# Loading the first six modulation pieces of each mixer into idle activation slots

## The chip, the core and the metric

The kernel runs on one core of one Trainium2 chip. A core has TensorE (PE in the profile; PEld is its weight load), VectorE (DVE), ScalarE (ACT), GpSimd (POOL) and SyncE (SP), each working through its own instructions in order; SP issues nearly nothing but DMAs. The metric is the device time of one execution in microseconds. Three runs of the kernel before gave 1124.48, 1122.46 and 1122.72 us: a median of 1122.72.

## The reference, cut to what matters

Two layers over 256 tokens of width 1024. Each has a mixer of three branches and an MLP, and each of these is modulated by six vectors (shift, scale and gate, for mixer and MLP) that come from one conditioning vector `c`:

```python
mod = jax.nn.silu(c) @ ada_w + ada_b
sh_m, sc_m, gt_m, sh_f, sc_f, gt_f = [t[:, None, :] for t in jnp.split(mod, 6, axis=-1)]

h = rms_norm(x, g_pre_mix) * (1.0 + sc_m) + sh_m
proj = h @ w_in
...
y_ret = jax.nn.silu(rg) * ret.reshape(B, S, RET_V)
y_lru = jax.nn.gelu(ly) * rg_lru(u, w_a, b_a, w_x, b_x, lam)
...
merged = g[:, :, 0] * (y_ret @ ret_w_o) + g[:, :, 1] * (y_lru @ lru_w_o) + g[:, :, 2] * (y_fox @ fox_w_o)
x = x + gt_m * rms_norm(merged @ w_out, g_post_mix)
h = rms_norm(x, g_pre_mlp) * (1.0 + sc_f) + sh_f
f = jnp.square(jax.nn.relu(h @ w1)) @ w2
return x + gt_f * rms_norm(f, g_post_mlp)
```

All is float32. A product with the 256 tokens is done on PE as three products of rounded parts (high x high, high x low, low x high). The product `silu(c) @ ada_w` has one row only and is not done on PE: DVE multiplies a tile of `ada_w` by `silu(c)` and sums it.

## The kernel before

**Pieces.** The weights come in pieces of 1 MiB (1024 x 256 numbers), each as two halves of 512 KiB, in the order of the list `ORDER`. A weight piece ("gemm") is loaded as two `wraw` tiles (`raw_half`, five slots in turn); ACT rounds each half to its high part (line 240) and DVE subtracts to get the low part (line 241), both into a `wpair` tile, of which there are four, that is two pieces. PE then runs 48 matmuls on it (lines 369 to 371). A modulation piece ("ada") is loaded through the same five `wraw` slots, and DVE sums each half in one instruction (line 301, `ada_sum`); a small add of the bias follows (line 297).

**Order in the mixer.** `mix_order` gives the weight pieces of a mixer; its end is rg x4, g1, w_r x4, g1, ly x4, then the last 28: fq, w_l x4, fv x4, fq x3, fk x4, g2 x4, w_f x4, w_o x4. In this document they are counted from 0 at the first of these `fq`, and from 0 within a name (`w_l0` to `w_l3`; `fq1` to `fq3` are pieces 9 to 11 of the 28). `weight_order` and its `spread` put the modulation pieces between them, evenly from the piece that stands `MIXR[l][0]` before the end to the one `MIXR[l][1]` before it. Layer 0 has 12 of them in its mixer (gt_m, sc_f, sh_f, four each), layer 1 has 8 (sc_f, sh_f). Before, layer 0 puts 12 pieces after pieces 6 to 18 of the last 28, and layer 1 puts 8 after pieces 8 to 18.

**What sets the time of a load.** `prefetch` keeps two weight pieces ahead of PE and runs the modulation steps that stand between them. All loads leave through SP's one queue, in order; a load waits on SP until the reader of its slot is done, and holds what is behind it. The framework's scheduler may move instructions of an engine against each other where data allows it, unless they are pinned with `keep_in_program_order`.

**Activation slots.** T1 to T10 are big activation tiles with changing tenants (`U(tag, ...)`). In the mixer T5 holds the retention output `ro_o` (read last in `ret_gate`), T6 `lru_u` (read last in `gelu_gate`), T7 `lru_t` and T8 `lru_a` (read last in `recurrence`). From `fk` on, T5 and T6 hold the keys `fkh` and `fkl`, T7 and T8 the output of that attention, `yfh` and `yfl`. Between the two tenants they are idle. In the opening, T slots already serve as homes for raw pieces (tile `wfirst`).

**PSUM.** The result of a piece lands in one of two banks of the pool `pg`; it is emptied by ACT and DVE (for `fv`, `fq` and `fk`: a rounding on ACT, then a subtraction on DVE into `fvl`, `fql` or `fkl`) before the piece after the next can start. The modulation columns that a norm needs are collected in `rcols` shortly before `w_f` ends.

Of the kernel before, what the change touches and what calls it, by code (L numbers as in the profile page):

```python
# [10 lines left out]
F32 = mybir.dt.float32  # L11
# [3 lines left out]
ALU = mybir.AluOpType  # L15
PSUM = bass.MemoryType.PSUM
KH = 4
# [16 lines left out]
P = 128  # L34
# [7 lines left out]
C = 256  # L42
# [5 lines left out]
PARTS = {'sh_m': 0, 'sc_m': 1, 'gt_m': 2, 'sh_f': 3, 'sc_f': 4, 'gt_f': 5}  # L48
# [21 lines left out]
def mix_order(l):  # L70
    first = 'g0 g0 g0 g0 lx lx g1 lx g1 lx lru' if l == 0 else \
            'rv rv rv rv rq rk g0 rq rk g0 lx g0 lx g0 lx g1 lx lru g1'
    rest = 'rg rg rg rg g1 w_r w_r w_r w_r g1 ly ly ly ly fq w_l w_l w_l w_l fv fv fv fv fq fq fq fk fk fk fk ' \
           'g2 g2 g2 g2 w_f w_f w_f w_f w_o w_o w_o w_o'
    order = first.split() + rest.split()
    return [(n, order[:i].count(n)) for i, n in enumerate(order)]


def mlp_order():
    w1 = lambda g: [('w1', 4 * g + c) for c in range(4)]  # L80
    w2 = lambda g: [('w2', 4 * g + c) for c in range(4)]
    return w1(0) + w1(1) + w2(0) + w1(2) + w2(1) + w1(3) + w2(2) + w2(3)
# [4 lines left out]
    return name in ('rv', 'w_o', 'w2') or (name == 'w1' and cix < 4)  # L87


MIXR = ((22, 8), (20, 8))  # L90
MLPR = ((5, 28), (5, 15))


def weight_order():
    order = [(n, 0, k) for k in range(KD) for n in ('ada_row', 'row')]

    def spread(l, gem, ada, lo, hi):
        at = [lo + (hi - lo) * i // max(len(ada), 1) for i in range(len(ada))]
        for i, (n, c) in enumerate(gem):
            order.append(('gemm', l, n, c))  # L100
            while at and at[0] <= i:
                at.pop(0)
                order.append(ada.pop(0))
        assert not ada

    for l in range(L):
        n = len(mix_order(l))
        parts = [(l, p) for p in ('gt_m', 'sc_f', 'sh_f')][l:]
        spread(l, mix_order(l), [('ada',) + p + (c,) for p in parts for c in range(4)], *(n - i for i in MIXR[l]))
        parts = [(l, 'gt_f')] + [(i, p) for i in range(l + 1, L) for p in ('sc_m', 'sh_m', 'gt_m')]  # L110
        spread(l, mlp_order(), [('ada',) + p + (c,) for p in parts for c in range(4)], *MLPR[l])
    return order


ORDER = weight_order()


@with_exitstack
def trunk_kernel(ctx, tc, x, c, vec, con, ffw, wts, out):
    nc = tc.nc  # L120
# [5 lines left out]
    sp = ctx.enter_context(tc.tile_pool(name="sp", bufs=2))  # L126
# [5 lines left out]
    V, A, T = nc.vector, nc.scalar, nc.tensor  # L132
# [4 lines left out]
    sir = cpool.tile([P, D], F32, name="sir")  # L137
# [11 lines left out]
    def vc(l, name):  # L149
        o, w = VEC[name]  # L150
        return vsb[:, l, o:o + w]
# [57 lines left out]
    pos = [0]  # L209

    def raw_half(i, extra=None):
        n = C if extra is None else C + NH_F
        t = wp.tile([P, KH, n], F32, name="wraw", tag="wraw", bufs=NRAW)
        src = wts[pos[0], i]
        if extra is None:
            nc.sync.dma_start(t.rearrange("p k c -> p (k c)"), src)
        else:
            nc.sync.dma_start(t[:, :, :C], src.rearrange("p (k c) -> p k c", k=KH))
            nc.sync.dma_start(t[:, :, C:], extra[:, i * KH:(i + 1) * KH, :])
        return t  # L220
# [25 lines left out]
    def load_split(l, name, cix):  # L246
        with ExitStack() as stack:
            if (name, cix) in LATE:
                for i in behind.pop(l, ()):
                    stack.enter_context(tc.issue_after(i))  # L250
            return split_of(l, name, cix)

    def split_of(l, name, cix):
        parts = []
        for i in range(2):
            t = early.pop(0) if early else raw_half(i, ffw[l] if (name, cix) == ('fv', 0) else None)
            n = t.shape[-1]
            if (name, cix) in SLOTS:
                own = SLOTS[name, cix][i]
            elif name in ('w1', 'w2') and (name, cix) < ('w2', 12):  # L260
                own = SPARE_SLOTS[spare[0] % len(SPARE_SLOTS)]
                spare[0] += 1
            else:
                own = PL
            broad = wide(name, cix)
            if own:
                hi, lo = halves_of(up.tile([P, 2 * D + SLOT_PAD], F32R, name="wown", tag=own), broad, 0 if broad else PHASE)
            else:
                hi, lo = split_tiles(broad, n)
            split(t, hi, lo)  # L270
            parts.append((hi, lo))
        pos[0] += 1
        if wide(name, cix):
            return [(parts[k // 2][0][:, k % 2, :], parts[k // 2][1][:, k % 2, :]) for k in range(KH)]
        return [(parts[k // KH][0][:, k % KH, :], parts[k // KH][1][:, k % KH, :]) for k in range(KD)]
# [20 lines left out]
    def mod_bias(l, o, n, src):  # L296
        V.tensor_tensor(mods[l][:, o:o + n], src, vc(l, 'ada_b')[:, o:o + n], ALU.add)

    def ada_sum(t, m):
        t = t.rearrange("p k c -> p (k c)")  # L300
        V.scalar_tensor_tensor(t, t, 0.5, sir, ALU.mult, ALU.mult, accum_out=m)  # L301

    def ada_step(l, part, cix):
        m = sp.tile([P, 2], F32, name="mcol")
        for j in range(2):
            ada_sum(raw_half(j), m[:, j:j + 1])
        pos[0] += 1
        mod_bias(l, PARTS[part] * 8 + 2 * cix, 2, m)

    ahead = []  # L310

    def prefetch(n=2):
        while len(ahead) < n and pos[0] < len(ORDER):
            o = ORDER[pos[0]]
            if o[0] == 'gemm':
                ahead.append((o[1:], load_split(*o[1:])))
            else:
                ada_step(*o[1:])

    def weight(l, name, cix):  # L320
        prefetch(3 if name in DEEP else 2)
        key, w = ahead.pop(0)
        assert key == (l, name, cix), (key, l, name, cix)
        return w
# [104 lines left out]
    def U(tag, shape, dt, name, other=False):  # L429

        o, n = PHASE * other, math.prod(shape[1:])
        t = up.tile([P, 2 * D + SLOT_PAD], dt, name=name, tag=tag)[:, o:o + n]
        dims = {c: k for c, k in zip("abc", shape[1:])}
        return t.rearrange(f"p ({' '.join(dims)}) -> p {' '.join(dims)}", **dims)
# [25 lines left out]
    def first_rows():  # L460
# [38 lines left out]
        def row_sums(k):  # L499
            m = sp.tile([P, 2], F32, name="mrow")  # L500
            for j in range(2):
                ada_sum(raws[2 * k][j], m[:, j:j + 1])
            return m
# [181 lines left out]
              'w_l': 1.7, 'fq': 2.4, 'fv': 2.4, 'fk': 2.4, 'g2': 3.0, 'w_f': 1.2, 'w_o': 1.0}  # L685

    def mixer(l, nm, h=None, rvp=None, qkp=None):
        hh, hl = h or nm.h

        def G(name, i, x=None, natural=False):  # L690
            prefetch(3 if name in DEEP else 2)
            side(BUDGET[name])
            w = weight(l, name, i)
            ps = pa.tile([P, 2, S], F32, name="ps", tag="a") if name in LONG else None
            return (gemm_n if natural else gemm)(w, *(x or (hh, hl)), ps)
# [151 lines left out]
        if rvp:  # L847
            for j in range(2):
                for t in range(2):
                    rv_evac(rvp[t][j], (2 * j, 2 * j + 1), (t, t))  # L850
                if j == 0:
                    prefetch(1)
        else:
            def rv_quad(ps, t, j):
                rv_evac(ps.rearrange("p (h c) -> p h c", h=2), (2 * j, 2 * j + 1), (t, t))
                return lambda: None

            first_quad(l, 'rv', nm, rv_quad)
# [281 lines left out]
    for l in range(L):  # L1140
        nm = mlp(l, mixer(l, nm) if l else mixer(l, None, *first_rows()))
# [101 lines left out]
```

## Time and profile before

| what | us |
|---|---|
| median of three runs | 1122.72 |
| the profiled execution, its own time | 1122.77 |
| span of the profiled execution, first to last instruction | 1121.0 |
| loads of 512 KB into `wraw`, issue to landing, median | 4.3 |
| line 301 on `wraw` tiles, 82 instructions | 100.0 |
| line 241 on `wpair` tiles, 286 instructions | 347.4 |

The profile shows one execution. "Busy" is the time that an engine's instructions cover; matmuls are pipelined, so that their durations (278 ns) overlap and one starts every 113 ns or so. A row of the timeline gives start, duration, engine and line, operation, output<-inputs and shapes, and in brackets how long the engine had been idle and what ended that. In the table of waits a row gives who waited for whom, the total in us, how many times, and the longest.

### The profile page before, as it was taken

The page shows a single profiled execution, that of the slowest core. Times are in us where ns is not written, and L with a number is a line of the kernel's source. Part 1 is how long each engine was busy: PE and PEld are TensorE (multiplying, and loading weights), DVE is VectorE, ACT ScalarE, POOL GpSimd, SP SyncE. Part 2 cuts the span into 40 slices and gives each one's busy share as a digit, 9 for nine tenths or more (in the row PEclk, how much of TensorE's full clock was granted, in tenths as well). Part 3 has the DMA queues.
Part 4 walks back from the last instruction along what each step waited for, and adds up shares of the span by engine and source line. Part 5 has one row for each costly group of instructions (what it writes and reads, how often), then busy time and mean ns, then how long its engine had stood idle before and what let it go on. Part 6 is the DMA issues. An engine that isn't in the chain of part 4 may idle for free.

```text
span 1121.0 us, 20568 instructions
## 1 busy us (share of the span) xinstructions
PE 1099.2 (98%) x8208; PEld 1037.1 (93%) x8208; DVE 870.5 (78%) x1324; ACT 617.4 (55%) x924; POOL 47.0 (4%) x62
## 2 busy tenths in 40 slices
PE   8999999999999999999999999999999999999997
PEld 7999999998899889989879999999999997989986
DVE  5998788878797789888487768887878778866543
ACT  5686595644355546445455657755445655544441
POOL 1001000000000110000030010000000003000000
PEclk9999999999999999999999999999999999999999
DMA  9954646678886569998735455566678584886541
GB/s 364 407 181 158 195 137 214 194 248 294 286 266 222 188 213 335 338 333 306 278 136 188 139 185 186 164 213 198 235 267 284 184 283 134 281 276 195 197 156 59
DMA packets 74284, 255.43 MB, mean 228 GB/s; under 512 B 10108, under 2 KB 12492, under 8 KB 74188
## 3 DMA queue, kind: packets, MB, share of 16 engines
q1 hardware_dynamic: 74188, 254.12, 66.5%
q8 instruction: 64, 1.05, 0.4%
q14 instruction: 32, 0.26, 0.1%
HBM read 253.00 MB, written 1.09 MB: 227 GB/s over the span
## 4 chain that ended last, share of the span: by engine, by line
PE 73%; DVE 9%; DMA 8%; issue 4%; ACT 3%; POOL 1%; SPq 0%; DVEq 0%; POOLq 0%; ACTq 0%
PE ps L371 22%; PE ps L369 21%; PE ps L370 21%; DMA wraw<-in_wts_dram 8%; DVE wpair L241 3%; DVE wraw L301 2%; ACT wpair L240 1%; POOL rs_v L198 1%; ACT junk L450 1%; POOL rs_r L199 1%; PE rvp L369 1%; PE rvp L370 0%; PE qkp L370 0%; PE qkp L371 0%; PE qkp L369 0%
## 5 line engine op out<-in xcount | busy, mean ns | idle before, releaser
L241 DVE TENSOR_TENSOR wpair<-wraw,wpair 128x1024 fp32r<-128x1024 f32 (+1 forms) x286 | 347.4, 1220 | 76.6 <-ACT wpair L240 74.7
L240 ACT CAST wpair<-wraw 128x1024 fp32r<-128x1024 f32 (+1 forms) x286 | 298.5, 1049 | 192.6 <-PE ps L371 128.7
L369 PE MATMUL ps<-hh,wpair 128*128 128x256 f32 x1312 | 364.4, 278 | 3.6 <-DVE fvl L701 2.6
L371 PE MATMUL ps<-hh,wpair 128*128 128x256 f32 x1312 | 362.9, 277 | 0.1
L370 PE MATMUL ps<-hl,wpair 128*128 128x256 f32 x1312 | 362.7, 276 | 0.0
L369 PEld LDWEIGHTS ps<-hh,wpair 128*128 128x128 f32 x1312 | 246.4, 188 | 4.7 <-DVE fvl L701 3.0
L371 PEld LDWEIGHTS ps<-hh,wpair 128*128 128x128 f32 x1312 | 246.3, 188 | 0.3 <-DVE wpair L241 0.3
L370 PEld LDWEIGHTS ps<-hl,wpair 128*128 128x128 f32 x1312 | 246.3, 188 | 0.2
L301 DVE SCALAR_TENSOR_TENSOR wraw<-wraw,sir 128x1024 f32<-128x1024 f32 x82 | 100.0, 1221 | 40.2 <-DMA wraw<-in_wts_dram 40.0
L241 DVE TENSOR_TENSOR wown<-wraw,wown 128x1024 fp32r<-128x1024 f32 x72 | 87.5, 1221 | 26.7 <-ACT wown L240 26.3
L240 ACT CAST wown<-wraw 128x1024 fp32r<-128x1024 f32 x72 | 74.8, 1048 | 55.9 <-DMA wraw<-in_wts_dram 30.3
L369 PE MATMUL ps<-wpair,mih 128*128 128x512 f32 x144 | 56.3, 391 | 0.0
L370 PE MATMUL ps<-wpair,mih 128*128 128x512 f32 x144 | 56.1, 389 | 0.0
L371 PE MATMUL ps<-wpair,mil 128*128 128x512 f32 x144 | 56.0, 389 | 0.0
L369 PE MATMUL ps<-wpair,hh 128*128 128x256 f32 (+1 forms) x144 | 45.6, 317 | 0.0
L370 PE MATMUL ps<-wpair,hh 128*128 128x256 f32 (+1 forms) x144 | 45.4, 316 | 0.0
L371 PE MATMUL ps<-wpair,hl 128*128 128x256 f32 (+1 forms) x144 | 45.4, 315 | 0.0
L369 PE MATMUL ps<-hh,wown 128*128 128x256 f32 x160 | 44.2, 276 | 0.0
L371 PE MATMUL ps<-hh,wown 128*128 128x256 f32 x160 | 44.2, 276 | 0.0
L370 PE MATMUL ps<-hl,wown 128*128 128x256 f32 x160 | 44.2, 276 | 0.0
L369 PE MATMUL ps<-wown,mih 128*128 128x512 f32 x112 | 43.7, 390 | 0.0
L370 PE MATMUL ps<-wown,mih 128*128 128x512 f32 x112 | 43.6, 389 | 0.0
(348 smaller groups left out, 2303.3 us busy)
## 6 DMA issues: line engine op xcount, KB each, us to landing
wraw<-in_wts_dram SPq DMA_DIRECT2D x440, 512.0 KB, 4.3
wfirst<-in_wts_dram SPq DMA_DIRECT2D x28, 512.0 KB, 10.2
rows<-drow SPq DMA_DIRECT2D x10, 512.0 KB, 6.1
xs<-in_x_dram SPq DMA_DIRECT2D x2, 512.0 KB
out_dram<-xs SPq DMA_DIRECT2D x4, 256.0 KB, 2.0
csb<-in_con_dram SPq DMA_DIRECT2D x1, 768.0 KB
csb<-in_con_dram SPq DMA_DIRECT2D x1, 256.0 KB, 9.6
vsb<-in_vec_dram SPq DMA_DIRECT2D x1, 152.0 KB, 6.5
```

The lines of the kernel that those rows point to most:

```text
L198: pin(nc.gpsimd.tensor_scalar(v, part, rest, None, ALU.add))
L199: nc.gpsimd.tensor_tensor(r, v, mhalf[:, :1], ALU.pow)
L240: copy(hi, t)
L241: V.tensor_tensor(lo, t, hi.bitcast(F32), ALU.subtract)
L301: V.scalar_tensor_tensor(t, t, 0.5, sir, ALU.mult, ALU.mult, accum_out=m)
L369: T.matmul(ps, ah, bh, start=start, stop=False, **kw)
L370: T.matmul(ps, ah, bl, start=False, stop=False, **kw)
L371: T.matmul(ps, al, bh, start=False, stop=stop, **kw)
L450: return A.activation(j, x, AF.Square, scale=D ** -0.5, accum_out=acc)
```

## The change

The first six modulation pieces of each mixer get a home in T5, T6, T7, T8, T5, T6 in turn. They stand in `ORDER` after pieces 0, 1, 2, 3, 7 and 9 of the last 28, and their sums are made, pinned on DVE, once the weight pieces 2, 4, 5, 7, 9 and 11 of the 28 have been split. The other six of layer 0 stay as they were in kind and come after pieces 10, 11, 13, 15, 16 and 18; the other two of layer 1 after pieces 15 and 17.

```diff
-MIXR = ((22, 8), (20, 8))
+MIXR = ((28, 8), (28, 8))
+PARK = ('T5', 'T6', 'T7', 'T8')
+PARK_FROM = 28
+PARK_AT = (0, 1, 2, 3, 7, 9)
+PARK_DUE = (2, 4, 5, 7, 9, 11)
...
-    def spread(l, gem, ada, lo, hi):
+    def spread(l, gem, ada, lo, hi, parked=0):
         at = [lo + (hi - lo) * i // max(len(ada), 1) for i in range(len(ada))]
+        if parked:
+            first = len(gem) - PARK_FROM
+            at[:parked] = [first + d for d in PARK_AT[:parked]]
+            ada[:parked] = [a + (PARK[i % 4], first + PARK_DUE[i]) for i, a in enumerate(ada[:parked])]
...
-    def ada_step(l, part, cix):
-        m = sp.tile([P, 2], F32, name="mcol")
-        for j in range(2):
-            ada_sum(raw_half(j), m[:, j:j + 1])
+    parked = []
+
+    def ada_step(l, part, cix, home=None, due=None):
+        if home:
+            t = U(home, [P, 2, KH, C], F32, "wada")
+            for j in range(2):
+                nc.sync.dma_start(t[:, j].rearrange("p k c -> p (k c)"), wts[pos[0], j])
+            raws = [t[:, j] for j in range(2)]
+        else:
+            raws = [raw_half(j) for j in range(2)]
         pos[0] += 1
-        mod_bias(l, PARTS[part] * 8 + 2 * cix, 2, m)
+
+        def sums():
+            m = sp.tile([P, 2], F32, name="mcol")
+            for j in range(2):
+                i = ada_sum(raws[j], m[:, j:j + 1])
+                if home:
+                    tc.keep_in_program_order(i)
+            mod_bias(l, PARTS[part] * 8 + 2 * cix, 2, m)
+
+        if home:
+            parked.append((due, sums))
+        else:
+            sums()
...
                 ahead.append((o[1:], load_split(*o[1:])))
+                gems[0] += 1
+                while parked and gems[0] > parked[0][0]:
+                    parked.pop(0)[1]()
```

The sequence of PE's instructions is the same before and after; those of SP and DVE move. On SP, around the last piece of `w_l` and the first of `fv` in layer 0 (the four `wraw` rows ahead of the first `in_ffw` row are `w_l2` and `w_l3`; `fv0` is the piece with the `in_ffw` columns), before:

```order
L216 DMA wraw_2726<-in_wts_dram 128x1024
L216 DMA wraw_2731<-in_wts_dram 128x1024
L216 DMA wraw_2788<-in_wts_dram 128x1024
L216 DMA wraw_2793<-in_wts_dram 128x1024
L218 DMA wraw_2850<-in_wts_dram 128x4x256
L219 DMA wraw_2850<-in_ffw_dram 128x4x8
L218 DMA wraw_2856<-in_wts_dram 128x4x256
L219 DMA wraw_2856<-in_ffw_dram 128x4x8
```

and after (`wada_2667` is the second modulation piece, A1, in T6; `wada_3076` the fifth, A4, the second tenant of T5):

```order
L225 DMA wraw_2739<-in_wts_dram 128x1024
L225 DMA wraw_2744<-in_wts_dram 128x1024
L225 DMA wraw_2804<-in_wts_dram 128x1024
L318 DMA wada_2667<-in_wts_dram 128x1024 x2
L225 DMA wraw_2809<-in_wts_dram 128x1024
L227 DMA wraw_2870<-in_wts_dram 128x4x256
L228 DMA wraw_2870<-in_ffw_dram 128x4x8
L318 DMA wada_3076<-in_wts_dram 128x1024
L227 DMA wraw_2876<-in_wts_dram 128x4x256
L228 DMA wraw_2876<-in_ffw_dram 128x4x8
```

The loads of A1 now stand between the halves of `w_l3`, and the first half of A4 between those of `fv0`. The pieces A0 (T5), A2 (T7) and A3 (T8) are issued much earlier, among the loads of the pieces that were read while `rg` to `ly` ran.

On DVE, layer 0, from the split of `fq3` to that of `fk0` (rows that read `wraw` and write `wpair` are splits, rows that write `mcol` are sums, `fql` rows empty a PSUM bank), before:

```order
L241 TENSOR_TENSOR wpair_3292<-wraw_3290,wpair_3292 128x4x256
L301 SCALAR_TENSOR_TENSOR wraw_3352,mcol_3351<-wraw_3352,sir_84 128x1024
L937 SCALAR_TENSOR_TENSOR fql_2602<-ps_3231,fqh_2601 128x512
L301 SCALAR_TENSOR_TENSOR wraw_3355,mcol_3351<-wraw_3355,sir_84 128x1024
L241 TENSOR_TENSOR wpair_3297<-wraw_3295,wpair_3297 128x4x256
L297 TENSOR_TENSOR mod0_110<-mcol_3351,vsb_83 128x2
L241 TENSOR_TENSOR wpair_3361<-wraw_3359,wpair_3361 128x4x256
L937 SCALAR_TENSOR_TENSOR fql_2602<-ps_3300,fqh_2601 128x512
```

and after:

```order
L250 TENSOR_TENSOR wpair_3298<-wraw_3296,wpair_3298 128x4x256
L306 TENSOR_TENSOR mod0_110<-mcol_3292,vsb_83 128x2
L969 SCALAR_TENSOR_TENSOR fql_2602<-ps_3237,fqh_2601 128x512
L250 TENSOR_TENSOR wpair_3303<-wraw_3301,wpair_3303 128x4x256
L310 SCALAR_TENSOR_TENSOR wada_3224,mcol_3306<-wada_3224,sir_84 128x1024 x2
L310 SCALAR_TENSOR_TENSOR wraw_3361,mcol_3365<-wraw_3361,sir_84 128x1024
L306 TENSOR_TENSOR mod0_110<-mcol_3306,vsb_83 128x2
L310 SCALAR_TENSOR_TENSOR wraw_3363,mcol_3365<-wraw_3363,sir_84 128x1024
L969 SCALAR_TENSOR_TENSOR fql_2602<-ps_3310,fqh_2601 128x512
L306 TENSOR_TENSOR mod0_110<-mcol_3365,vsb_83 128x2
L250 TENSOR_TENSOR wpair_3371<-wraw_3369,wpair_3371 128x4x256
```

Between the two `fql` rows there were one half sum and two splits; now there are four half sums (A5 from T6, A7 from `wraw`) and one split.

More of the change, by code (lines that the diff above doesn't have):

```diff
@@ L108, in weight_order @@
         parts = [(l, p) for p in ('gt_m', 'sc_f', 'sh_f')][l:]
-        spread(l, mix_order(l), [('ada',) + p + (c,) for p in parts for c in range(4)], *(n - i for i in MIXR[l]))
+        spread(l, mix_order(l), [('ada',) + p + (c,) for p in parts for c in range(4)], *(n - i for i in MIXR[l]),
+               parked=6)
         parts = [(l, 'gt_f')] + [(i, p) for i in range(l + 1, L) for p in ('sc_m', 'sh_m', 'gt_m')]
@@ L300, in ada_sum @@
         t = t.rearrange("p k c -> p (k c)")
-        V.scalar_tensor_tensor(t, t, 0.5, sir, ALU.mult, ALU.mult, accum_out=m)
-    def ada_step(l, part, cix):
-        m = sp.tile([P, 2], F32, name="mcol")
-        for j in range(2):
-            ada_sum(raw_half(j), m[:, j:j + 1])
-        pos[0] += 1
-        mod_bias(l, PARTS[part] * 8 + 2 * cix, 2, m)
+        return V.scalar_tensor_tensor(t, t, 0.5, sir, ALU.mult, ALU.mult, accum_out=m)
+    parked = []
[7 more added lines that the diff above has]
+            raws = [raw_half(j) for j in range(2)]
+        pos[0] += 1
+        def sums():
[9 more added lines that the diff above has]
+            sums()
     ahead = []
+    gems = [0]
     def prefetch(n=2):
@@ L687, in mixer @@
     def mixer(l, nm, h=None, rvp=None, qkp=None):
+        gems[0] = len(ahead)
         hh, hl = h or nm.h
```

## The prediction

> **What bounds the kernel now.** I read the page first, then the busy time of each engine by stretches, then who waited for whom inside the stretch that the change touches.
>
> ```profile
> span 1121.0 us, 20568 instructions
> PE 1099.2 (98%) x8208; PEld 1037.1 (93%) x8208; DVE 870.5 (78%) x1324; ACT 617.4 (55%) x924; POOL 47.0 (4%) x62
> PE   8999999999999999999999999999999999999997
> ```
>
> TensorE (PE) is busy for 98% of the span, so the kernel is bound by its matmuls, and whatever is to be won lies in the 21.8 us in which PE stands still. The change keeps PE's order as it is, so it can gain only where PE waits. Both layers run the same mixer code; I therefore cut the same stretch out of each, from the first matmul of `w_l` (it reads ylh) to the first of `w_f` (it reads yfh). These four rows of the timeline give the cuts, and the busy table gives what lies between them (us, then busy time and instructions of PE, PEld, DVE, ACT and POOL, the granted clock, the share of the DMA engines and GB/s).
>
> ```profile
> 215.68 0.28 PE L369 MATMUL ps<-ylh,wpair 128*128 128x256 f32 x1
> 344.10 0.36 PE L369 MATMUL ps<-yfh,wpair 128*128 128x256 f32 x1
> 769.12 0.28 PE L369 MATMUL ps<-ylh,wpair 128*128 128x256 f32 x1
> 889.47 0.36 PE L369 MATMUL ps<-yfh,wpair 128*128 128x256 f32 x1
> ...
> 215.68:344.10 128.42, 121.90 (x1043) 120.00 (x1042) 103.80 (x217) 59.92 (x101) 0.00 (x0) 1.00 0.78 258
> 769.12:889.47 120.35, 120.22 (x1044) 119.63 (x1042) 94.92 (x195) 59.70 (x100) 0.00 (x0) 1.00 0.71 240
> ```
>
> The same matmuls take 128.42 us in layer 0 and 120.35 us in layer 1: **8.07 us** more. PE idles 6.52 us in the first and 0.13 us in the second; the other 1.5 us is the pace that PE loses around each stop. What differs is the number of modulation sums (line 301) in the stretch, and how long VectorE (DVE) waits for their data:
>
> ```profile
> 215.68:344.10 128.42, 29.49 (x48) 1.00 0.78 258
> 769.12:889.47 120.35, 19.64 (x32) 1.00 0.71 240
> ...
> DVE wraw L301 <- DMA wraw<-in_wts_dram: 14.6, 13, 2.5
> ...
> DVE wraw L301 <- DMA wraw<-in_wts_dram: 9.9, 7, 2.6
> ```
>
> The first two rows are line 301 alone; each sum is followed by a short read of the accumulator, so x48 is 24 half pieces, 12 pieces, and x32 is 8 pieces. The two rows of waits are layer 0 (14.6 us in 13 waits) and layer 1 (9.9 us in 7). How such a wait reaches PE is seen here:
>
> ```profile
> 264.93 1.23 DVE L301 SCALAR_TENSOR_TENSOR wraw<-wraw,sir 128x1024 f32<-128x1024 f32 x1 [0.69 <-DMA wraw<-in_wts_dram]
> ...
> 266.56 1.23 DVE L301 SCALAR_TENSOR_TENSOR wraw<-wraw,sir 128x1024 f32<-128x1024 f32 x1 [0.39 <-DMA wraw<-in_wts_dram]
> 267.71 0.08 DVE L301 DVE_READ_ACCUMULATOR wraw<-wraw,sir 128x1 f32 x1
> 267.71 0.69 DVE L701 TENSOR_TENSOR fvl<-ps,fvh 128x512 fp32r<-128x512 f32 x1
> 268.31 1.22 DVE L241 TENSOR_TENSOR wpair<-wraw,wpair 128x1024 fp32r<-128x1024 f32 x1
> ...
> 268.45 0.38 PE L369 MATMUL ps<-hh,wpair 128*128 128x256 f32 x1 [1.15 <-DVE fvl L701]
> ```
>
> DVE works in order. Two sums stood in front of the subtraction that empties a PSUM bank (`fvl`), both waiting for their transfers, and PE waited 1.15 us for that bank. The transfers were late because they share five `wraw` slots with the weights: a piece of weights takes two slots, so does a modulation piece, and a slot is refilled only when DVE has read it.
>
> **The change part by part.** *Work.* Nothing is computed more or less: 12 and 8 pieces are summed as before, with the same instruction on a tile of the same shape. That the tile lies in a T slot has a direct measure in the opening, where fourteen halves of modulation pieces did so:
>
> ```profile
> L301 DVE SCALAR_TENSOR_TENSOR wraw<-wraw,sir 128x1024 f32<-128x1024 f32 x82 | 100.0, 1221 | 40.2 <-DMA wraw<-in_wts_dram 40.0
> L301 DVE SCALAR_TENSOR_TENSOR wfirst<-wfirst,sir 128x1024 f32<-128x1024 f32 x14 | 16.9, 1220 | 1.6 <-DMA wfirst<-in_wts_dram 1.6
> ```
>
> 1221 against 1220 ns: no cost.
>
> *Slots, layer 0.* Call the pieces A0 to A11. A0 to A5 go to T5 to T8 and leave the five slots to the weights. A6 to A11 still use them, after weight pieces 10, 11, 13, 15, 16 and 18 of the last 28. The sums from the fourth piece of `fv` on are then eight: A4 and A5 (parked) and A6 to A11. Layer 1 of before has eight sums in the same part (after pieces 8, 9, 11, 12, 14, 15, 17, 18), all eight through `wraw`, and PE idles 0.13 us. So layer 1 of before is my measure for layer 0 of after: **-8.07 us**.
>
> *Sums that move forward.* A0 to A3 are summed between `w_l0` and `fv2`, where DVE had none. Row of the first three of these pieces, with two rows used further down:
>
> ```profile
> 215.68:231.97 16.29, 16.29 (x146) 16.29 (x145) 11.41 (x14) 7.02 (x8) 0.00 (x0) 1.00 0.64 200
> ...
> 20.00:40.00 20.00, 18.37 (x117) 16.22 (x116) 17.44 (x24) 13.90 (x23) 0.00 (x0) 1.00 1.03 409
> 440.00:460.00 20.00, 20.00 (x90) 16.54 (x90) 17.10 (x26) 8.71 (x9) 0.00 (x0) 1.00 0.98 349
> ```
>
> One weight piece takes PE 16.29 / 3 = 5.43 us. DVE is idle for 16.29 - 11.41 = 4.88 us there, and the four half sums of A0 and A1 need 4 x 1.22 = 4.88 us. Queued behind a pinned pair of sums (2.44 us) are the next piece's split and the evacuation of a bank; the split is wanted only a piece later and the bank again one piece after its matmuls end, so a delay of up to 2.44 us against 5.43 us costs nothing. Bounds: 0 to 2.44 us for each of the eight pairs A0 to A3 in both layers, 19.5 us in all; I take 0.
>
> *The tightest place.* Between the end of `fv2` and the start of `fk0` PE has four pieces, 21.7 us. The order of after gives DVE there A4, A6, A5 and A7 (eight half sums), six splits and four evacuations. In the rows above they follow each other at 1.15 us (266.56 to 267.71) and 0.60 us (267.71 to 268.31): 14 x 1.15 + 4 x 0.60 + 0.3 for small ones = 18.8 us. The first evacuation must wait for ScalarE's half of it:
>
> ```profile
> 254.60 0.59 ACT L944 CAST fvh<-ps 128x512 fp32r<-128x512 f32 x1
> ```
>
> With 0.6 us for that and 0.5 us (a guess) for the hand-overs, 1.8 us remain. It fits; I allow **+0.3 us**.
>
> *The SP queue.* All loads leave through one in-order queue, so a parked load that waits for its slot holds the weights behind it. T5 is read last at line 918 and T7 and T8 at lines 748 and 751, both over 25 us before `w_l0`. The late one is T6: A1 stands between the two halves of `w_l3` and waits for the last `gelu_gate` (line 929).
>
> ```profile
> L918 DVE TENSOR_TENSOR th<-th,ro_o x4: 680/686/693, 134.9 to 154.2; 128x512 f32<-128x512 f32 x4
> ...
> L751 DVE TENSOR_TENSOR_SCAN lru_u<-lru_a,lru_u x8: 664/680/684, 171.6 to 187.3; 128x256 f32<-128x256 f32 x8
> ...
> 213.32 0.33 SPq L216 DMA_DIRECT2D wraw<-in_wts_dram  x1
> ...
> 215.78 0.33 SPq L216 DMA_DIRECT2D wraw<-in_wts_dram  x1
> ...
> 213.93 0.69 DVE L929 TENSOR_TENSOR ge<-ge,lru_u 128x512 f32<-128x512 f32 x1
> ```
>
> The halves are issued at 213.32 and 215.78, since the second waits for a `wraw` slot; T6 is free at 214.62, in between. Cost 0, with 1.2 us to spare. The second load of T5 (A4) stands between the halves of `fv0` and waits for the sums of A0:
>
> ```profile
> 217.65 1.22 DVE L241 TENSOR_TENSOR wpair<-wraw,wpair 128x1024 fp32r<-128x1024 f32 x1 [0.44 <-ACT wpair L240]
> ...
> 220.98 0.56 SPq L218 DMA_DIRECT2D wraw<-in_wts_dram  x1
> ...
> 232.20 1.08 ACT L240 CAST wpair<-wraw 128x1056 fp32r<-128x1056 f32 x1 [1.64 <-PE ps L371]
> ```
>
> Those sums follow the first row, so they end at about 217.65 + 3 x 1.15 = 221.1, 0.1 us after the second half of `fv0` was issued; that half is cast only at 232.20, so a hold of even a few us costs 0. A5 and the sums of A1 are the same case two pieces on. Each parked sum is due two to five pieces (11 to 27 us) after its load, against 4.8 us to land:
>
> ```profile
> wraw<-in_wts_dram SPq DMA_DIRECT2D x63, 512.0 KB, 4.8
> ```
>
> So the new wait of DVE for a parked tile costs 0 (if a load took over 11 us, DVE would stand and PE after it).
>
> *Layer 1.* Its stretch has 0.13 us of PE idle to give: **-0.1 us**.
>
> *Sum.* -8.07 + 0.3 - 0.1 = -7.9 us. The profiled execution took 1122.77 us, 1.8 us beyond its span of 1121.0, and the median is 1122.72. The span goes to 1113.1 and the time to **1114.8 us**.
>
> **The rivals.** *DVE is the next bound (1118.8).* The tight place has 1.8 us to spare only if A6 and A7 find their data. If their four halves wait as in layer 0 now, 14.6 / 13 = 1.1 us each, PE loses 4.5 - 1.8 = 2.7 us, and half of that again at A9 and A10, which also stand close: 4.0 us, hence 1118.8. For it: twice as many sums there as before. Against it: layer 1 lets DVE wait 9.9 us without PE noticing.
>
> *The transfers are the bound (1115.8).* The bytes stay, and from `fq2` to `fk1` they are dense: four weight pieces and A6, A7, A8, 7 x 1.049 = 7.3 MB in 21.7 us, or 338 GB/s. This stretch moved 258 GB/s at a share of 0.78, which is 331 at a full share: 22.2 us, 0.5 us late, and once more for A9 and A10: +1.0 us. Against it: 349 GB/s held for 20 us with PE at 20.00, and 409 near the start. [...]
>
> *It does not help (1122).* Layer 0 might be slow not from late data but because it has four more sums, 9.85 us of DVE work, close to the 8.07 us. Parking moves that work and removes none. Against it: 14.6 us of DVE's idle time there was waiting for those tiles, and 103.80 us of work in 120.35 us is 86%, no full engine.
>
> *Slower (1124.6).* The sums A0 to A3 land where DVE's idle time just covers them (4.88 against 4.88). If they pushed splits and evacuations back so far that PE had to wait, up to 19.5 us would come in over both layers. The gain is eaten when over 7.9 / 19.5 = 40% of it shows; at half, 9.75 - 7.9 = 1.9 us are lost: 1124.6. Against it: the delay of one pair is under half a piece, and no sum waits.
>
> **How the numbers follow.** Forecast 0.68; DVE next 0.18; transfers 0.04; no help 0.05; slower 0.05. About 0.2% (2.2 us) can be told from no change, so faster is 0.90, same 0.05, slower 0.05. The range runs from 1113.5 to 1118.8: below, each stretch also sheds a little over half a us of the slack around softmax (x1044 at 16.29 / 146 = 0.112 us is 117 us of the 120.35); above, the first rival in full. That leaves out the last two cases and a little of the tails.
>
> **What would show it.** Right: the layer 0 stretch at about 120.6 us, PE's waits for fvl, fql, fkl and sm gone, line 301 on parked tiles never waiting for DMA, layer 1 at 120.2. Wrong: PE waiting for fql or for a split around `fk0` (DVE next), the landings above 6 us (transfers), sums with no wait and PE still idle (no help), or PE idle between `w_l0` and `fv2` (slower); a gap between the halves of `w_l3` on SP would be the T6 wait.

## The result and the profile after

The changed kernel took 1113.19 us (median of three runs, 1112.68 to 1113.91) against 1122.72 us: 9.5 us less, a ratio of 0.9902 with an interval of 0.9881 to 0.9923. Measured again, on another occasion with five rounds, it took 1114.17 us against 1123.07, a ratio of 0.9929 (0.9915 to 0.9942). So it is faster by 0.7 to 1.0%; the forecast was 1114.8 us, which is a ratio of 0.9930, and the range began at 1113.5.

From the page of the kernel after: the span, the busy line, PE's busy tenths, the sums that still use the slots (busy us, mean ns, idle time ahead of them), and the two kinds of load (512 KB each, median us to landing).

```profile
span 1110.9 us, 20557 instructions
PE 1096.3 (99%) x8208; PEld 1036.3 (93%) x8208; DVE 872.0 (78%) x1324; ACT 617.7 (56%) x924; POOL 46.2 (4%) x62
PE   8999999999999999999999999999999999999997
...
L310 DVE SCALAR_TENSOR_TENSOR wraw<-wraw,sir 128x1024 f32<-128x1024 f32 x58 | 70.8, 1222 | 22.5 <-DMA wraw<-in_wts_dram 22.3
...
wraw<-in_wts_dram SPq DMA_DIRECT2D x416, 512.0 KB, 4.3
wada<-in_wts_dram SPq DMA_DIRECT2D x24, 512.0 KB, 5.3
```

The profiled execution took 1112.68 us, 1.8 us beyond its span, as before; the span is 10.1 us shorter. PE now stands still for 1110.9 - 1096.3 = 14.6 us of it, where it was 21.8 us. DVE's work has not changed (870.5 and 872.0 us). Line numbers have moved: the sums of line 301 are line 310, ACT's rounding 240 is 249, the split 241 is 250, the matmuls 369 to 371 are 400 to 402, and 701 and 937 (the evacuations) are 733 and 969.

The same cut as in the prediction, from the first matmul on ylh to the first on yfh, in the busy table of the kernel after; layer 0, then layer 1.

```profile
214.85:334.63 119.78, 119.73 (x1044) 119.46 (x1042) 104.12 (x217) 60.16 (x101) 0.00 (x0) 1.00 0.74 251
759.57:879.35 119.78, 119.73 (x1044) 119.46 (x1042) 95.76 (x195) 60.07 (x100) 0.00 (x0) 1.00 0.65 216
```

Both layers take 119.78 us, to the hundredth, with PE busy for 119.73 of them: a **floor**. Layer 0 has lost 8.64 us, layer 1 0.57 us. The remaining 0.83 us come from ahead of both: the first matmul that reads yrh started at 161.28 us before and at 160.45 us now. That part is the same in both kernels, over the profiles below it varied from 160.09 to 163.18 us, and a second trace of before has it at 160.37 us, so nothing ties those 0.83 us to the change.

In the list of waits of the same two stretches (us in total, times, longest) PE no longer appears: its waits for fvl, fql, fkl and sm are gone. Two of them in layer 0 of before, then what is left after of DVE's wait for modulation data, layer 0 and layer 1:

```profile
PE ps L369 <- DVE fvl L701: 2.6, 2, 1.4
...
PE ft L997 <- DVE sm L991: 1.9, 2, 1.1
...
DVE wraw L310 <- DMA wraw<-in_wts_dram: 4.6, 3, 2.5
...
DVE wraw L310 <- DMA wraw<-in_wts_dram: 2.2, 2, 1.9
```

DVE's wait was 14.6 and 9.9 us. The view of the tile `wada` alone (the parked pieces of both layers) shows how their sums fared:

```profile
L310 DVE SCALAR_TENSOR_TENSOR wada<-wada,sir x24: 1217/1220/1223, 218.0 to 813.4; 128x1024 f32<-128x1024 f32 x24
...
its engine sat idle before it (us, times) until:
who waited for it (us, times):
  ACT wpair L249: 3.3, 2
...
DMA to landing us min/median/max: 4.1/5.3/7.3
```

Nothing stands under "sat idle before it": of 24 sums on parked tiles none waited for its load, although loads took up to 7.3 us. ACT waited twice behind parked sums, PE never.

### The profile page after: what moved, and what is told of

Read it like the earlier page. It is cut to its first block, busy times and chain, and to the rows that moved or that the text cites. A ratio compares the mean times of both kernels' runs of the same rounds, so it can differ in the third digit from the quotient of the medians.

```text
span 1110.9 us, 20557 instructions
## 1 busy us (share of the span) xinstructions
PE 1096.3 (99%) x8208; PEld 1036.3 (93%) x8208; DVE 872.0 (78%) x1324; ACT 617.7 (56%) x924; POOL 46.2 (4%) x62
## 3 DMA queue, kind: packets, MB, share of 16 engines
q8 instruction: 64, 1.05, 0.4%
## 4 chain that ended last, share of the span: by engine, by line
PE 85%; DVE 6%; ACT 3%; issue 2%; DMA 2%; POOL 1%; SPq 0%; POOLq 0%; DVEq 0%; ACTq 0%
PE ps L402 25%; PE ps L400 25%; PE ps L401 25%; DVE wpair L250 2%; ACT wpair L249 1%; POOL rs_v L207 1%; DMA wraw<-in_wts_dram 1%; POOL rs_r L208 1%; ACT junk L481 1%; PE rvp L400 1%; PE rvp L401 0%; PE qkp L401 0%; PE qkp L400 0%; PE qkp L402 0%; PE rvp L402 0%
## 5 line engine op out<-in xcount | busy, mean ns | idle before, releaser
L250 DVE TENSOR_TENSOR wown<-wraw,wown 128x1024 fp32r<-128x1024 f32 x72 | 87.5, 1222 | 25.2 <-ACT wown L249 24.8
L310 DVE SCALAR_TENSOR_TENSOR wraw<-wraw,sir 128x1024 f32<-128x1024 f32 x58 | 70.8, 1222 | 22.5 <-DMA wraw<-in_wts_dram 22.3
```

The lines of the kernel that those rows point to most:

```text
L250: V.tensor_tensor(lo, t, hi.bitcast(F32), ALU.subtract)
L310: return V.scalar_tensor_tensor(t, t, 0.5, sir, ALU.mult, ALU.mult, accum_out=m)
```

## The experiments

The table has what every run gave: its time (median, or the one run), the ratio to the kernel before with its interval where there were rounds, the two stretches, and DVE's total wait for modulation halves in each. "Before" is the first trace. In one trace a stretch is one sample; single times also carry the opening (the part ahead of the first matmul on yrh), which varied by 3 us.

| run | us | ratio | layer 0 | layer 1 | DVE's waits |
|---|---|---|---|---|---|
| before | 1122.72 | | 128.42 | 120.35 | 14.6 / 9.9 |
| b0_before | 1121.63 | | 127.57 | 120.91 | 14.1 / 11.8 |
| after | 1113.19 | 0.9902 (0.9881 to 0.9923) | 119.78 | 119.78 | 4.6 / 2.2 |
| a0_after | 1114.17 | 0.9929 (0.9915 to 0.9942) | 120.63 | 119.78 | 6.1 / 1.5 |
| e1_spread | 1121.58 | 0.9988 (0.9977 to 0.9999) | 126.65 | 122.19 | 18.7 / 15.3 |
| e2_park | 1117.51 | 0.9952 (0.9939 to 0.9966) | 122.56 | 121.17 | 6.9 / 11.7 |
| e3_slots6 | 1122.42 | | 122.22 | 124.45 | 9.9 / 15.3 |
| e8_share5 | 1124.83 | | 128.82 | 121.56 | 15.2 / 11.4 |
| e5_late | 1125.03 | 1.0022 (1.0008 to 1.0036) | 133.74 | 119.77 | 0 / 0 |
| e6_soon | 1115.53 | 0.9937 (0.9922 to 0.9953) | 121.74 | 119.77 | 7.0 / 1.4 |
| e7_layer1 | 1121.20 | 0.9984 (0.9972 to 0.9995) | 127.83 | 119.77 | 13.9 / 1.9 |
| e4_twice | 1115.09 | 0.9933 (0.9915 to 0.9950) | 121.39 | 119.78 | 0.2 / 2.4 |
| e9_wide | 1116.90 | 0.9954 (0.9939 to 0.9968) | 123.29 | 119.77 | 13.7 / 3.9 |

**Both kernels again.** The changed kernel and, later, the kernel before were profiled a second time without an edit.

> The changed kernel again, unaltered. Both theories: stretch w_l to w_f 119.8 us in both layers (before: 128.4 and 120.4), time 1113 us, 9.2 to 9.6 us under before. It also asks whether the 0.8 us that the opening (first instruction to the first matmul on yrh, 161.28 us before, 160.45 us after) lost in the profile belongs to the change: if it is chance from execution to execution, the opening may come out anywhere between 160.4 and 161.3 us here, since no instruction of it differs.

> The kernel before once more, for a second trace of it: how far its two stretches (128.42 and 120.35 us in the first trace) repeat. If the wait for late loads depends on where each load happens to land, they move by half a us or more from trace to trace (layer 1 to 120.3 to 121.3 us, layer 0 to 127.5 to 129 us) while a stretch that has reached its floor of matmul time does not; if layer 1 of before was a floor with 0.13 us of idle PE, as the prediction took it, it repeats within 0.2 us.

The second trace of before, layer 0 and layer 1, in the busy table:

```profile
214.77:342.34 127.57, 121.80 (x1043) 120.02 (x1042) 103.65 (x217) 59.78 (x101) 0.00 (x0) 1.00 0.78 260
767.35:888.26 120.91, 120.36 (x1044) 119.63 (x1042) 94.73 (x195) 59.91 (x100) 0.00 (x0) 1.00 0.72 239
```

Layer 1 of before does not repeat: 120.35, 120.91 and, with the same code in e2_park, 121.17 us. It was no floor, and the prediction took it for one. Layer 1 of after repeats to 0.01 us. Layer 0 of after does not quite (119.78 and 120.63 us): there PE still waited 0.6 us for ptl in one trace.

**Is it the spreading or the homes?** The list of `MIXR` now begins 28 pieces off the end in both layers, so the sums are also spread more evenly. This kernel has the spreading alone:

```diff
-               parked=6)
+               parked=0)
```

> Spread alone: the modulation pieces of a mixer are spread evenly over 20 weight pieces (28 to 8 before its end) and none is parked; all go through the five wraw slots. Theory S (late data: the five slots are asked for 2 halves a weight piece plus 2 for each modulation piece, and in layer 0 of before that was nearly 4): now 12 in 20 is 3.2 halves a piece, about what layer 1 of before had (8 in 12, 3.3) at 120.4 us, so layer 0 stretch about 120.4 us, layer 1 about 119.8 us, time 1113.5 to 1114 us; parking itself would be worth under 1 us. Rival K (the home outside the slots is what counts): layer 0 stretch stays at 124 us or more, time 1118 us or more. Rival D (the count of DVE sums in the crowded part): also about 120 us, so this run does not tell S from D.

It measured 1121.58 us: the spreading alone gives next to nothing at this density; layer 1 even loses, and DVE waits longer than before. (Spreading wider does give something; see the last run.) How one of these waits comes about is seen in layer 1 of this run, in the timeline (start, duration, engine, line; in brackets the idle time before it and what ended it):

```profile
815.78 1.21 DVE L250 TENSOR_TENSOR wpair<-wraw,wpair 128x1024 fp32r<-128x1024 f32 x1
...
817.02 0.33 SPq L225 DMA_DIRECT2D wraw<-in_wts_dram  x1
...
822.44 1.23 DVE L310 SCALAR_TENSOR_TENSOR wraw<-wraw,sir 128x1024 f32<-128x1024 f32 x1 [4.31 <-DMA wraw<-in_wts_dram]
823.59 0.08 DVE L310 DVE_READ_ACCUMULATOR wraw<-wraw,sir 128x1 f32 x1
823.59 0.69 DVE L969 SCALAR_TENSOR_TENSOR fql<-ps,fqh 128x512 fp32r<-128x512 f32 x1
...
824.33 0.39 PE L400 MATMUL ps<-hh,wpair 128*128 128x256 f32 x1 [0.67 <-DVE fql L969]
```

A split ends at about 817.0 us and frees a slot; at 817.02 us SP issues the load of the modulation half into it. DVE has only one more split to do (the two end at 818.1) and stands at the sum until 822.44 us, when the half is there, 5.4 us after its issue. Behind the sum waits the evacuation `fql`, and behind that PE. The load leaves **because** DVE has come this far, and the sum stands so close behind in DVE's order that DVE arrives at it before the data. That closeness is the framework's choice: by the kernel's order of instructions DVE takes this sum ahead of the splits of three weight halves whose loads left earlier (at 812.94, 814.09 and 815.22 us). The order of before shows the same: `wraw_3352` is summed ahead of the split of `wraw_3295`, which was loaded first (their loads left at 266.19 and 264.27 us). No run pins the sums behind those splits and changes nothing else.

**Is it the work of the sums or their waits?** Layer 0 alone parked, with the loads early but the sums at the pieces of before, so that DVE has the same work in the same stretch:

```diff
-MIXR = ((28, 8), (28, 8))
+MIXR = ((22, 8), (20, 8))
-PARK_AT = (0, 1, 2, 3, 7, 9)
-PARK_DUE = (2, 4, 5, 7, 9, 11)
+PARK_AT = (0, 1, 2, 3, 8, 9)
+PARK_DUE = (6, 7, 8, 9, 10, 11)
-               parked=6)
+               parked=6 if l == 0 else 0)
```

> Parking alone, in layer 0 only: six pieces are loaded early into T5 to T8, but their sums stand where before had them (after pieces 6 to 11 of the last 28), and the other six pieces and all of layer 1 stay as before. Theory S: the waits of the first six pieces go, those of the last six (one to each weight piece from 13 to 18) stay: layer 0 stretch 123 to 125 us, time 1117 to 1119 us. Rival D (DVE's work in the crowded part is what costs): nothing changes in DVE's work or place, so 128 us and 1122.5 us. Layer 1: 120.4 us by both.

Layer 0 came down to 122.56 us, the time to 1117.51 us. DVE's busy time in the stretch is that of before (third busy figure here; 103.80 us then), its wait for modulation data fell from 14.6 to 6.9 us:

```profile
215.64:338.20 122.56, 120.49 (x1044) 119.58 (x1042) 103.69 (x217) 60.03 (x101) 0.00 (x0) 1.00 0.73 245
...
DVE wraw L310 <- DMA wraw<-in_wts_dram: 6.9, 6, 1.9
```

So some two thirds of layer 0's loss (5.9 of 8.6 us, in one trace) are late data and not DVE's work; the rival "It does not help" falls.

**A sixth slot.** The kernel before with six `wraw` slots; to make room, temporaries share single buffers. The second run shares them too, but keeps five slots.

```diff
-NRAW = 5
+NRAW = 6
...
-            sq = tmp("t0", "sq")
+            sq = tmp("ul", "sq", bufs=1)
...
-            ch = tmp("ch", "ch", F32R, (P, S), bufs=1)
+            ch = tmp("uh", "ch", F32R, (P, S), bufs=1)
```

> The kernel before, with its order of loads, and a sixth wraw slot; the room for it comes from letting the temporaries of tag t0 and ch share single buffers with ul and uh, which may slow the retention heads and the norms outside the stretch. So only the stretch w_l to w_f is read. Theory S: data come earlier by up to a fifth, layer 0 stretch 120 to 124 us, DVE's waits for DMA before sums under 8 us (before 14.6 us). Rival D: 128 us as before, whatever the slots.

> The shared temporaries of the run with six slots, but with the five slots of before: what the sharing alone costs. If the sharing is what spoiled layer 1 there (124.45 us), layer 1 comes out at 123 us or more here too and layer 0 at 128.5 us or more, so that the sixth slot by itself gave more than the 6 us that layer 0 showed; if the sixth slot itself spoiled layer 1, both layers stay within 0.7 us of before (127.7 to 129.1 and 119.8 to 121.1 us).

With six slots layer 0 took 122.22 us, layer 1 124.45 us; with five and the sharing, 128.82 and 121.56 us. The sharing costs 0.4 to 1.3 us in each against the two traces of before, so it is not what spoiled layer 1: the sixth slot takes 6.6 us off layer 0 and, against what was expected, adds 2.9 us to layer 1 (one trace each). DVE's waits in layer 0 fell to 9.9 us, not under 8, and with the sharing alone layer 1 came out 0.5 us above the band given for it. That a slot more only shifts which half waits for which split is a reading that these two traces do not prove; why layer 1 gets worse was not followed further.

**Late sums without homes.** The kernel of the spreading alone (the lines taken out here are its own), every piece through the shared slots, but its sums pinned behind the split of the next weight piece:

```diff
+        elif late:
+            ada = [a + (None, d + 1) for a, d in zip(ada, at)]
...
-                if home:
+                if due is not None:
                     tc.keep_in_program_order(i)
...
-        if home:
+        if due is not None:
             parked.append((due, sums))
...
-               parked=0)
+               late=True)
```

> The even spread again, with every modulation piece through the five shared slots, but its two sums pinned behind the split of the NEXT weight piece. Theory Lead (what PE loses comes from sums that DVE reaches before their load has landed, because the load leaves only when a split just ahead frees a slot): one more weight piece, 5.4 us, between load and sum is enough, so DVE's waits for modulation halves in the two stretches fall from 18.7 and 15.3 us to under 3 us each, the stretches to 120 to 121.5 us, the time to 1114 to 1116.5 us. Theory Held slots (the shared slots themselves are what is short, and a piece that stays in two of the five for one weight piece longer starves the weights): stretches at or above 126.6 and 122.2 us, time 1121 us or more.

Neither theory has all of it. DVE's waits for modulation data are gone in both layers, and layer 1 stands at the floor. Layer 0 is the worst of all runs, though this trace is of the slowest execution of the kernel (1130.09 us, median 1125.03). Its busy row, what ACT's rounding of the weights waited for there (52.2 us) and PE for that rounding; then the same wait of ACT in layer 0 of before (24.5 us); then the busy row of layer 1 and ACT's wait there:

```profile
217.49:351.23 133.74, 124.82 (x1043) 122.08 (x1042) 104.03 (x215) 61.69 (x103) 0.00 (x0) 0.99 0.73 247
...
ACT wpair L251 <- DMA wraw<-in_wts_dram: 52.2, 24, 5.6
...
PE ps L402 <- ACT wpair L251: 2.0, 2, 1.3
...
ACT wpair L240 <- DMA wraw<-in_wts_dram: 24.5, 11, 5.1
...
777.00:896.77 119.77, 119.72 (x1044) 119.44 (x1042) 95.24 (x193) 60.74 (x101) 0.00 (x0) 1.00 0.72 241
...
ACT wpair L251 <- DMA wraw<-in_wts_dram: 27.7, 14, 4.5
```

A piece that waits for its sum in two of five slots takes them from the weights. With the eight pieces of layer 1 that is borne: ACT waits longer there too, but PE does not. With twelve in the same 20 weight pieces it is not: the weights come late instead, and PE waits for their rounding and splits (4.1 us in all). So at this density a late sum cures the one wait and causes the other, unless the piece lies elsewhere; late sums with fewer pieces in layer 0 were not run.

**Homes with less delay.** The changed kernel, each parked piece to be summed sooner. The code looks at the parked sums only when a weight piece has just been split, so with this edit a sum stands behind the split of the next weight piece, not (as the text below has it) right behind the one it follows. That is one piece of delay, as in e5_late; the changed kernel has two to four:

```diff
-PARK_DUE = (2, 4, 5, 7, 9, 11)
+PARK_DUE = PARK_AT
```

> The changed kernel with its homes in T5 to T8, but each parked piece summed right behind the weight piece that it follows in the load order, no 2 to 5 pieces later. Lead: a load into a home of its own need not wait for a split, so it leaves well ahead of the sum in any case and the delay adds little; also A5 and A4 are summed earlier and the tight place is looser: stretches 119.7 to 121 us, DVE's waits for parked tiles under 2 us in all, time 1113 to 1115 us. Rival Delay (the homes alone do nothing, the late sum is what gives the time): DVE waits for parked tiles about 1 us for each half, 10 us or more in layer 0, stretches 122 to 126 us, time 1117 to 1121 us.

1115.53 us, between the two expectations; layer 1 at the floor, layer 0 at 121.74 us. No parked tile waited for its load; all 7.0 us of DVE's waits in layer 0 are pieces that still use the slots:

```profile
214.91:336.65 121.74, 120.04 (x1044) 119.56 (x1042) 103.92 (x215) 61.01 (x102) 0.00 (x0) 1.00 0.74 246
...
DVE wraw L310 <- DMA wraw<-in_wts_dram: 7.0, 5, 3.8
```

The homes carry the gain: with one piece of delay e5_late has layer 0 at 133.74 us without homes, and this run has 121.74 us with them for the first six pieces (the other six are not delayed here). The further delay of one to three pieces is worth 1 to 2 us in layer 0 by these traces, and nothing that the ratios tell apart (0.9937 with 0.9922 to 0.9953 against 0.9929 with 0.9915 to 0.9942). Homes with no delay at all were not run.

**Layer 1 alone.**

```diff
-MIXR = ((28, 8), (28, 8))
+MIXR = ((22, 8), (28, 8))
-               parked=6)
+               parked=6 * l)
```

> The change in layer 1 alone, layer 0 as before. The prediction's own step (layer 1 has 0.13 us of PE idle to give): 1122.6 us, ratio above 0.999. Rival Pace (the idle time of PE is only part of what it loses around its stops, so layer 1 gives what its stretch showed, 120.35 or 121.17 us in two runs of the same code against 119.78): 0.6 to 1.4 us, 1121.4 to 1122.1 us, layer 1 at 119.8 us and layer 0 at 127 to 129 us.

The ratio is 0.9984 (0.9972 to 0.9995), 0.6 to 3.1 us: layer 1 does give something. By the stretches it is 0.6 to 1.4 us (119.77 against 120.35 to 121.17); layer 0 with the code of before took 127.83 us.

**How tight is the tight place?** The sums of A4 and A5 in layer 0 done twice, into a column that is not used:

```diff
+TWICE = (('sc_f', 0), ('sc_f', 1))
...
+                if home and l == 0 and (part, cix) in TWICE:
+                    x = sp.tile([P, 2], F32, name="mtwice")
+                    tc.keep_in_program_order(ada_sum(raws[j], x[:, j:j + 1]))
```

> The changed kernel with the four half sums of the two parked pieces in the tight place (A4 and A5, between the end of fv2 and the start of fk0 in layer 0) done twice, 4 x 1.22 = 4.9 us more for DVE there. The prediction's reckoning (1.8 us of margin, whatever is over it comes out of PE): layer 0 at about 122.9 us, time 1117 us. Rival Slack (evacuations and splits may run late by most of a piece, and DVE catches up behind fk0): PE loses under 1 us, layer 0 at or below 121.3 us, time at or below 1115 us.

Layer 0 took 121.39 us, 0.8 to 1.6 us above the two traces of after, although DVE worked 4 us more (108.25 against 104.12 us). PE's one long stop, for a split at the end of the place:

```profile
217.57:338.96 121.39, 119.95 (x1044) 119.48 (x1042) 108.25 (x225) 60.02 (x101) 0.00 (x0) 1.00 0.74 247
...
280.79 0.38 PE L406 MATMUL ps<-hh,wpair 128*128 128x256 f32 x1 [1.38 <-DVE wpair L251]
```

Of the 4 x 1.22 = 4.9 us put in, 3.3 to 4.1 us were absorbed. The margin there is about twice the 1.8 us of the prediction; layer 0 and the time lie within 0.1 us of what the rival Slack allowed. DVE caught up behind the place: its waits for modulation data in layer 0, 4.6 and 6.1 us in the two traces of after, fell to 0.2 us.

**Spread wider instead.** No homes, no late sums, the pieces over weight pieces 44 to 8 from the end:

```diff
-MIXR = ((28, 8), (28, 8))
+MIXR = ((44, 8), (44, 8))
-               parked=6)
+               parked=0)
```

> No homes and no late sums: all pieces through the five shared slots, spread over weight pieces 44 to 8 from the mixer's end in both layers, so that a modulation piece follows only every third weight piece in layer 0 and six of the twelve stand ahead of w_l. Lead (each sum through the shared slots can still find its load in flight, but with two more weight pieces between two of them the slots recover): DVE's waits in the layer 0 stretch halve to under 8 us, that stretch 120 to 122 us, what is lost ahead of it under 1 us, time 1114 to 1117 us. Rival Home (only a place outside the slots takes the wait away, however thin the pieces are spread): layer 0 stretch above 124 us or as much lost ahead of w_l (the 54.4 us between the first matmuls that read yrh and ylh grow by over 2 us), time above 1118 us.

1116.90 us: the time is within what Lead gave, the layer 0 stretch lies between the two expectations, and DVE's waits there did not halve. The ratio of 0.9954 is about half to two thirds of the gain of the changed kernel (0.9902 and 0.9929), without any home. Layer 1 reaches the floor this way as well. In layer 0 half of the pieces now stand ahead of `w_l` (the part ahead grew from 54.40 to 54.67 us), and yet DVE waits nearly as long as before for the six that are left, up to 4.5 us for one:

```profile
216.50:339.79 123.29, 121.07 (x1044) 120.00 (x1042) 94.03 (x189) 61.70 (x104) 0.00 (x0) 1.00 0.68 225
...
DVE wraw L310 <- DMA wraw<-in_wts_dram: 13.7, 6, 4.5
```

DVE has 10 us less to do than in e6_soon and PE takes 1.5 us longer. Thinner pieces wait no less; there are only fewer of them. This spacing with late sums, which might do without homes, was not run. No run here beats the changed kernel; with both stretches at 119.78 us in its first trace there is no idle PE left in them to win.

## Why the prediction came out as it did

**The mechanism was right.** Late modulation data held DVE, DVE held the evacuations, these held PE; pieces with a home of their own take that away. e2_park (same work, less waiting), e6_soon against e5_late (the same delay, with homes and without) and the lists of waits show that homes are enough; that they are needed is not shown. Three of the forecast's four signs were met: PE's waits for fvl, fql, fkl and sm gone, no parked sum waiting, layer 0 at 119.8 to 120.6 us against 120.6. The fourth, layer 1 at 120.2 us, was not: it came to 119.78. The size was short: the span shrank by 10.1 us where 7.9 were reckoned.

- *Slots, layer 0* (-8.07): -8.64 us in the first trace, -7.8 us (128.42 to 120.63) in the second. The yardstick, layer 1 of before, was not where PE ends up.
- *Layer 1* (-0.1): **this step failed.** It read the idle time of PE, 0.13 us, as all that could be had, and -0.57 us came. The prediction itself had said for layer 0 that PE loses pace beside its idle time, and did not apply it here (that pace was 8.07 - 6.39 = 1.7 us, rather than 1.5, once layer 1's own 0.13 us of idle time is taken off); 9.9 us of DVE waits in that stretch were a second sign. In three traces this stretch lay 0.6 to 1.4 us above its floor. This error counts twice, since the same stretch was the measure for layer 0: 0.47 us of the shortfall here, 0.57 us there.
- *The tightest place* (+0.3): nothing in the first trace. DVE runs through it nearly without a gap, as reckoned (18.8 us); the 0.5 us for hand-overs in that sum was a guess that no run shows. The timeline of after, with the row before the first sum and the last splits of the place:

```profile
255.34 1.23 DVE L250 TENSOR_TENSOR wpair<-wraw,wpair 128x1024 fp32r<-128x1024 f32 x1 [0.26 <-ACT wpair L249]
256.48 1.22 DVE L310 SCALAR_TENSOR_TENSOR wada<-wada,sir 128x1024 f32<-128x1024 f32 x1
...
268.72 1.22 DVE L310 SCALAR_TENSOR_TENSOR wada<-wada,sir 128x1024 f32<-128x1024 f32 x1
...
269.87 1.22 DVE L310 SCALAR_TENSOR_TENSOR wraw<-wraw,sir 128x1024 f32<-128x1024 f32 x1
...
272.23 0.69 DVE L969 SCALAR_TENSOR_TENSOR fql<-ps,fqh 128x512 fp32r<-128x512 f32 x1
...
272.90 2.35 DVE L250 TENSOR_TENSOR wpair<-wraw,wpair 128x1024 fp32r<-128x1024 f32 x2
```

  A7 (the `wraw` row at 269.87) finds its data: by the order of the kernel its two loads left at 261.24 and 262.97 us, over 8 us before their sums, and the sums of A5 took 2.3 us of that. So the waits that the rival "DVE is the next bound" (1118.8 us) needed did not come about; e4_twice shows that a margin was there too.
- *Work* (0) and *Sums that move forward* (0): right. A sum takes 1220 ns on a parked tile and 1222 ns on a slot, and PE is busy for all but 0.05 us of the stretch.
- *The SP queue* (0): right. A1's loads and the second half of `w_l3`, in the timeline of after:

```profile
213.86 0.80 SPq L318 DMA_DIRECT2D wada<-in_wts_dram  x2
214.95 0.33 SPq L225 DMA_DIRECT2D wraw<-in_wts_dram  x1
```

  That half was issued when a split freed its slot, 0.3 us behind the loads of A1, and not later for them (it was at 215.78 before).
- *The transfers* (rival, 1115.8 us): some parked loads took over 6 us, which was named as its sign, but the shortest time from the issue of a parked load to its sum was 14.5 us (A1, 213.86 to 228.40 us), so a load of 7.3 us costs nothing. The sign was badly chosen. (By its own lists the sums stand two to four pieces behind their loads' place, not two to five.)
- *Slower* (rival, 1124.6 us): no part of it was seen.

The profiled span shrank by 2.2 us more than reckoned (10.1 against 7.9): 0.8 us are the opening, 0.9 us layer 0 with the allowance for the tight place (8.64 against 7.77), 0.5 us layer 1. The lower end of the range had allowed each stretch a little over half a us, and the two stretches alone (9.21 us) lead to 1122.72 - 9.21 = 1113.5 us, just that end. What takes the median of 1113.19 us another 0.3 us below it is no larger than the scatter of the opening, so that last step has no cause that a run shows; the repeat, 1114.17 us, lies inside the range, 0.6 us below the forecast.

## What to carry to other kernels

When a load leaves only because an in-order engine has just freed its buffer, and the load's reader stands close behind in that engine's order, the engine can reach the reader before the data, and everything behind the reader waits: in e1_spread the data were there 5.4 us after the issue, DVE stood for 4.31 us and PE behind it for 0.67 us. Here, spreading such loads within the crowded part gave next to nothing (a ratio of 0.9988), and moving half of them ahead of it (0.9954) gave about half to two thirds of the gain; a buffer that does not belong to the same ring gave the most (0.9902 and 0.9929), and delaying the reader helped only as long as the held buffers were not what the main stream lives on (e5_late: layer 1 119.77 us, layer 0 133.74 us). And a small idle time, 0.13 us in layer 1 of before, does not make a stretch a floor: here the floor showed in lengths that came back within 0.02 us in layer 1 of seven traces of six kernels (119.77 and 119.78 us). Take the measure for a forecast from such a stretch.

## What the runs showed of the hardware

In e5_late a stop of PE cost more than its length: PE stood for 1.98 us ahead of a matmul at 325.10 us; for the next 3.4 us the granted clock was 0.50, and matmuls of 128x256 started every 0.21 us where they start every 0.12 us afterwards. In the timeline, and in the busy table of that stretch and of the one behind it:

```profile
325.10 0.54 PE L1007 MATMUL fs<-ch,sel 128*128 128x256 f32 x1 [1.98 <-DVE mx L1016]
...
325.65 0.41 PE L403 MATMUL fs<-fkl,fqh 128*128 128x256 f32 x1
325.86 0.41 PE L404 MATMUL fs<-fkh,fql 128*128 128x256 f32 x1
...
328.71 0.28 PE L402 MATMUL ps<-hh,wpair 128*128 128x256 f32 x1
328.83 0.28 PE L403 MATMUL ps<-hl,wpair 128*128 128x256 f32 x1
...
325.10:328.50 3.40, 3.40 (x16) 3.40 (x17) 3.09 (x11) 3.22 (x11) 0.00 (x0) 0.50 0.94 307
328.60:333.00 4.40, 4.40 (x41) 4.40 (x40) 2.79 (x6) 1.50 (x2) 0.00 (x0) 1.00 0.57 212
```

Sixteen matmuls instead of some 29: about 1.5 us on top of the stop, while PE counts as busy. In e1_spread a stop of 2.19 us, which ended at 292.18 us, was followed by a slow spell too: the granted clock was 0.68 over the next 3.40 us and 0.56 over the 1.40 us behind them. After 1.05 us in e5_late and 1.7 us in e7_layer1 the clock stayed at 1.00. The busy table behind the stop of e1_spread, behind the one of 1.05 us in e5_late and behind the one of e7_layer1:

```profile
292.20:295.60 3.40, 3.40 (x20) 3.40 (x21) 3.40 (x6) 0.00 (x0) 0.00 (x0) 0.68 0.74 228
295.60:297.00 1.40, 1.40 (x9) 1.40 (x8) 1.40 (x7) 0.00 (x0) 0.00 (x0) 0.56 1.02 328
...
320.49:322.50 2.01, 2.01 (x17) 2.01 (x18) 2.01 (x3) 1.06 (x1) 0.00 (x0) 1.00 0.73 234
...
261.10:263.00 1.90, 1.90 (x16) 1.90 (x17) 1.90 (x7) 1.06 (x1) 0.00 (x0) 1.00 0.85 285
263.00:265.00 2.00, 2.00 (x20) 2.00 (x19) 1.93 (x3) 0.00 (x0) 0.00 (x0) 1.00 0.97 356
```

What sets off such a spell, these traces do not show.
